# A decoder layer's middle stage: combination slots claimed early, three gate blocks kept on chip, the gating root by Newton steps, later key fetches and weights one step ahead

## The chip, the core and the metric

The kernel runs on one core of one Trainium2 chip. Its engines are TensorE (PE, with PEld for its weight loads), VectorE (DVE), ScalarE (ACT), GpSimd (POOL) and SyncE (SP), whose queue issues nearly all DMAs. The metric is the device time of one execution in microseconds (us), the median of several runs.

## What is computed

One layer of a decoder over 1024 prompt positions and 32 sample rows (8 sequences of 4), all in float32, width 1024. Shortened from the reference:

```python
h = layer_norm(ALPHA * x + 0.5 * swiglu(x, f1_w1, f1_w3, f1_w2), ln1_g, ln1_b)
z = h @ w_in + b_in                       # q, k, v, uv, ga, gb: 42 blocks of 128 columns
for g, (window, dil) in enumerate(ATT_GROUPS):      # (128,1), (512,4), (2048,16), 4 heads each
    o, lse = dilated_attn(q_g, k_g, v_g)
att = combine_groups(outs, lses)          # softmax over the three groups' lse, per head
u, vr = split(gelu(uv))                   # 512 columns each
vn = layer_norm(vr, sgu_ln_g, sgu_ln_b)   # these rows of the sample are an output too
yb = u * (tril(ws) @ vn + sgu_b)          # chunks of 128 positions, 4 channel groups
mix = (sigmoid(ga) * (att @ w_oa) + sigmoid(gb) * (yb @ w_ob)) @ w_out
h = layer_norm(ALPHA * h + mix, ln2_g, ln2_b)
h = layer_norm(ALPHA * h + 0.5 * swiglu(h, f2_w1, f2_w3, f2_w2), ln3_g, ln3_b)
```

Outputs are the two results, the key and value windows, and the normalised rows `vn` of the sample.

## The kernel before

Activations lie transposed, 128 channels on the partitions and 1056 positions along the row, cut into four chunks of 264 columns (`NC`, `C`). Every float32 matmul is made of three in a rounded format: high times high, high times low, low times high (`mm3`, L236; the matmul itself is L240). `split` makes the high half by a ScalarE copy (L251) and the low half by a VectorE subtraction (L252).

A tile framework orders the instructions of each engine. It traces the program in the order of the code, then schedules each engine with a machine model, by priorities that follow the code; `high_priority(offset=URGENT)` moves an instruction 300 places ahead, `issue_after` puts it behind another on its engine. Waits between engines are semaphores. Tiles come from pools with a fixed number of slots that are reused: `S` (37 slots of up to 1056 columns), `W` (8, weights), `M` (6, staging), `R` and `Q` (2 each, raw data), `X` (small ones), and in PSUM `mm` (3 banks) and `ax` (5). A tile holds a slot from its first use to its last. `held` (L105) takes an `S` tile and has GpSimd copy one element per partition into it at once (L108), so that it has its slot from then on.

Three work queues run beside the main loop: `bg` (attention), `slow` (the sample's attention, `sample`) and `mid` (gating and combination). They hold Python generators; `tick(n, m)` after each block of matmuls runs n steps of `bg`, m of `slow` and three (`MID`) of `mid`, always of the first generator in a queue, until it ends.

The stages are `ffn` (first SwiGLU), `widen` (the wide projection; spills its blocks to DRAM, `zD`), `mix`, and `ffn` again. The change is in `mix` and what it runs:

- The main loop computes the last ten of the gates' sixteen blocks, `n` = 6 to 15 (`gate8`, L984; 24 matmuls a chunk; ScalarE adds the bias into an `M` tile, L990; the tile is stored to `zD`, L991). For `n` = 6 to 12 each block's weights are fetched (`unit`, L214 to L223) and all four chunks done. The last three blocks are fetched together and only chunks 0 to 2 done; chunk 3 comes later in `beside` (L1588), to fill TensorE.
- `attend(i)` (`bg`) runs six steps, two head pairs by three groups. It fetches q, k, v (`fetch_qkv`, `fetch_z`, L1138), turns v (L1180), and over eight blocks does scores (PE L1200, DVE L1208, ACT L1212), turning (L1223, L1227) and values (L1239). It fetches the next step's q, k, v near its start. Its row minima and sums go to DRAM (`mlD`, L1265).
- `combine(hp)` (`mid`) after three steps reads these back (L1283 to L1289, `raw`), computes each group's factor (L1297 to L1310), writes it to DRAM (`cD`, L1312), reads it broadcast into three tiles `cbs` (L1319), and scales and adds the groups into `att` (L1324 to L1327).
- `sgu_norm` (`mid`) takes the statistics of the four `vr` blocks, the reciprocal root (`rsqrt`, L659 to L663), the scaling of nine tiles (L1483), and the sample's output rows (L1488 to L1490). `sgu_mix` makes the gated `yb` (L1507 to L1520).
- Then come `local(n)`, eight blocks of `yb @ w_ob` (`product`, multiplied on VectorE into the gate `mt[n]`, L1541), and the last loop, eight blocks of `att @ w_oa`, multiplied into the gate `ta[n]` that `fetch_gate` (L1580) reads back, added (L1633) and split. Weights are fetched by `narrow` (L225 to L234).

Of the kernel before, what the change touches and what calls it, by code (L numbers as in the profile page):

```python
# [21 lines left out]
P = 128  # L22
# [59 lines left out]
class Trunk:  # L82
# [1071 lines left out]
    def attend(self, i):  # L1154
# [19 lines left out]
        self.fetch_qkv(i + 1)  # L1174
# [97 lines left out]
    def combine(self, hp):  # L1272
        nc = self.nc
        t = []
        raw = self.S([16, 3, 2, P])
        for g in range(3):
            x = raw[:, g]
            for m in range(2):
                for h in range(2):
                    src = self.mlD[hp, g, m, h]  # L1280
                    o = x[8 * h : 8 * h + 8, m]
                    if g == 0:
                        nc.sync.dma_start(o, src.rearrange("(a x) -> a x", a=8))  # L1283
                    elif g == 1:
                        nc.sync.dma_start(
                            o.rearrange("p (r b) -> p r b", r=4), src.rearrange("(r a b) -> a r b", r=4, a=8)
                        )
                    else:
                        nc.sync.dma_start(  # L1289
                            o.rearrange("p (r b) -> p r b", r=16), src.rearrange("(r a b) -> a r b", r=16, a=8)  # L1290
                        )
# [22 lines left out]
        att = self.S([P, NT])  # L1314
        self.att[hp] = att
        cbs = [self.S([P, NP]) for _ in range(3)]
        for g, cb in enumerate(cbs):
            for h in range(2):
                nc.sync.dma_start(cb[64 * h : 64 * h + 64], self.cD[hp, g, h].partition_broadcast(64))  # L1319
        yield from self.pause(3)  # L1320
        for g, cb in enumerate(cbs):
            aT = self.attT.pop((hp, g))
# [113 lines left out]
    def sgu_norm(self):  # L1436
# [28 lines left out]
        for i in range(9):  # L1465
# [19 lines left out]
        v = self.M([NS, 512])  # L1485
        for op, k in ((ALU.mult, "sgu_ln_g"), (ALU.add, "sgu_ln_b")):
            t = self.M([NS, 512])
            nc.sync.dma_start(t, a[k].partition_broadcast(NS))  # L1488
            nc.vector.tensor_tensor(v, vn[4][:NS, 0] if op == ALU.mult else v, t, op=op)
        nc.sync.dma_start(a["svo"], v)  # L1490
        self.vn = vn
# [32 lines left out]
    def mix(self):  # L1524
# [18 lines left out]
        def local(n):  # L1543
            wb = self.narrow(a["wo"][n, :, 2 * P :], 4 * P)
# [12 lines left out]
        sgu = [self.sgu_norm()] + [self.sgu_mix(gg) for gg in range(4)]  # L1557
# [288 lines left out]
```

## Time and profile before

| what | us |
|---|---|
| median of 3 runs | 2202.6 |
| lowest and highest | 2198.51, 2202.74 |
| the profiled execution, its own time | 2202.1 |
| its span, first to last instruction | 2200.3 |

| engine | busy us | share of the span |
|---|---|---|
| PE | 2132.7 | 97% |
| PEld | 2093.7 | 95% |
| DVE | 1555.3 | 71% |
| ACT | 892.8 | 41% |
| POOL | 321.6 | 15% |

How to read the lines: in a timeline, a row has its start, its length, the engine, the line of the code, the operation, output and input tiles without their numbers and, in brackets, how long the engine was idle before it and what ended the wait. `x24` means that 24 alike in a row are merged. `SPq` is SP's own queue: such a row is the issue of a DMA, not its transfer. In a table of waits, the numbers are the total in us, how often, and the longest. A busy TensorE is not one at full speed: the granted clock stands beside it. A row of groups has the count, busy us and mean ns, then the idle time before them with its main causes.

### The profile page before, as it was taken

How to read it: one execution, taken by the hardware profiler on the slowest of the kernel's cores; microseconds unless marked ns; L12 is line 12 of the kernel's file. 1: busy time of each engine (PE TensorE's matmuls, PEld its weight loads, DVE VectorE, ACT ScalarE, POOL GpSimd, SP SyncE). 2: the span in 40 equal slices, each digit the busy share in tenths (PEclk: the TensorE clock that was granted, in tenths of full speed). 3: DMA queues.
4: the chain of work that ended last, by engine and by line, in shares of the span. 5: the costliest groups of instructions: out<-in, count | busy, mean ns of one | idle time of the engine just before them, and what ended most of it. 6: DMA issues, size and time to landing. Idle time of an engine off the chain costs nothing.

```text
span 2200.3 us, 43275 instructions
## 1 busy us (share of the span) xinstructions
PE 2132.7 (97%) x17305; PEld 2093.7 (95%) x17305; DVE 1555.3 (71%) x2724; ACT 892.8 (41%) x1681; POOL 321.6 (15%) x234
## 2 busy tenths in 40 slices
PE   9999999999998999999989988999999999999997
PEld 8999999999998999999879877999999999999997
DVE  8776776656788726787674647778576777656887
ACT  5444444421225634344465453245344444421224
POOL 0432332200010022232000000000332233100000
PEclk9999999999999999999999998999999999999998
DMA  4435545598973325666854637514354454597841
GB/s 157 146 134 178 176 161 175 194 372 319 329 279 134 136 101 193 205 219 222 312 166 151 186 119 244 195 41 143 129 185 156 166 185 159 181 393 290 303 183 79
DMA packets 170553, 429.01 MB, mean 195 GB/s; under 512 B 24864, under 2 KB 61584, under 8 KB 167664
## 3 DMA queue, kind: packets, MB, share of 16 engines
q1 hardware_dynamic: 169920, 425.71, 55.1%
q8 instruction: 135, 2.21, 0.4%
q14 instruction: 66, 0.54, 0.1%
q10 hardware_dynamic: 432, 0.54, 0.1%
HBM read 305.56 MB, written 166.81 MB: 215 GB/s over the span
## 4 chain that ended last, share of the span: by engine, by line
PE 83%; DMA 7%; DVE 6%; ACT 2%; issue 1%; SPq 1%; POOL 0%; ACTq 0%; DVEq 0%; POOLq 0%
PE ax L240 44%; PE mm L240 35%; DMA M<-kv 3%; DMA zD<-M 1%; DVE W L252 1%; PE ax L1200 1%; DMA S<-zD 1%; DVE X L1382 1%; PE ax L1223 1%; DVE S L252 1%; PE ax L1239 0%; DVE M L1392 0%; DVE S L627 0%; DVE M L1381 0%; DVE X L1397 0%
## 5 line engine op out<-in xcount | busy, mean ns | idle before, releaser
L240 PE MATMUL mm<-S,W 128*128 128x264 f32 x5208 | 694.8, 289 | 30.1 <-DVE S L1541 13.2
L240 PE MATMUL ax<-S,W 128*128 128x264 f32 x5400 | 706.9, 284 | 0.4 <-DVE W L252 0.2
L240 PEld LDWEIGHTS mm<-S,W 128*128 128x128 f32 x5208 | 659.2, 191 | 46.8 <-DVE S L1541 15.2
L240 PEld LDWEIGHTS ax<-S,W 128*128 128x128 f32 x5400 | 677.0, 188 | 2.7 <-ACT S L1030 0.8
L240 PE MATMUL ax<-S,S 128*128 128x264 f32 x3240 | 478.7, 285 | 4.0 <-DVE S L1039 3.9
L240 PEld LDWEIGHTS ax<-S,S 128*128 128x128 f32 x3240 | 429.6, 189 | 5.3 <-DVE S L1039 5.3
L240 PE MATMUL mm<-S,S 128*128 128x264 f32 x2472 | 383.8, 285 | 2.6 <-DVE S L252 2.0
L240 PEld LDWEIGHTS mm<-S,S 128*128 128x128 f32 x2472 | 333.7, 188 | 4.3 <-DVE S L252 2.2
L251 ACT CAST W<-R 128x1024 fp32r<-128x1024 f32 (+3 forms) x173 | 128.8, 761 | 319.7 <-PE mm L240 137.4
L382 POOL TENSOR_TENSOR Q<-R 128x512 f32<-128x512 f32 x49 | 70.3, 1434 | 798.2 <-DMA R<-w13a 202.8
L252 DVE TENSOR_TENSOR W<-R,W 128x1024 fp32r<-128x1024 f32 (+3 forms) x173 | 152.1, 883 | 26.7 <-ACT W L251 22.2
L251 ACT CAST W<-Q 128x1024 fp32r<-128x1024 f32 (+1 forms) x78 | 76.8, 984 | 224.2 <-POOL Q L383 89.4
L816 DVE SCALAR_TENSOR_TENSOR S<-ax,S 128x264 f32<-128x264 f32 x240 | 99.4, 427 | 66.8 <-PE ax L240 65.7
L457 DVE TENSOR_TENSOR S<-ax,M 128x264 f32<-128x264 f32 x82 | 32.8, 432 | 151.3 <-PE ax L240 151.3
L108 POOL CAST S<-ones 128x1 fp32r<-128x1 f32 x32 | 17.6, 571 | 751.4 <-DVE S L1633 363.5
L252 DVE TENSOR_TENSOR S<-Q,S 128x1024 fp32r<-128x1024 f32 (+1 forms) x78 | 112.6, 1444 | 3.8 <-ACT S L251 3.8
L252 DVE TENSOR_TENSOR W<-Q,W 128x1024 fp32r<-128x1024 f32 (+1 forms) x78 | 89.6, 1149 | 26.6 <-ACT W L251 26.6
L251 ACT CAST S<-Q 128x1024 fp32r<-128x1024 f32 (+1 forms) x78 | 76.8, 984 | 68.1 <-PE ax L240 49.7
L251 ACT CAST S<-R 128x512 fp32r<-128x512 f32 (+1 forms) x64 | 44.1, 689 | 105.9 <-DMA sumsA<-S 39.4
L252 DVE TENSOR_TENSOR S<-S,M 128x528 fp32r<-128x528 f32 x72 | 84.5, 1174 | 2.6 <-ACT M L251 0.8
L383 POOL TENSOR_TENSOR Q<-Q,R 128x512 f32<-128x512 f32 x49 | 81.0, 1653 | 2.7
L390 POOL TENSOR_TENSOR Q<-R,Q 128x512 f32<-128x512 f32 x49 | 80.5, 1644 | 1.1
(204 smaller groups left out, 2049.6 us busy)
## 6 DMA issues: line engine op xcount, KB each, us to landing
ws<-st SPq DMA_DIRECT2D x144, 256.0 KB
S<-sumsA SPq DMA_DIRECT2D x63, 528.0 KB
S<-sumsB SPq DMA_DIRECT2D x63, 528.0 KB
M<-kv SPq DMA_DIRECT2D x96, 256.0 KB
sumsA<-M SPq DMA_DIRECT2D x90, 264.0 KB
sumsB<-M SPq DMA_DIRECT2D x90, 264.0 KB
R<-w13b SPq DMA_DIRECT2D x44, 512.0 KB
R<-w13a SPq DMA_DIRECT2D x42, 512.0 KB
```

Source lines behind the costliest of these rows:

```text
L108: self.nc.gpsimd.tensor_copy(t[:, 0, :1] if len(shape) == 3 else t[:, :1], self.ones[:, :1])
L240: mm = lambda a, b, s, e: nc.tensor.matmul(o, a[:, cc], b, start=s, stop=e, skip_group_check=True)
L251: a = self.nc.scalar.copy(hi, src)
L252: b = self.nc.vector.tensor_tensor(lo, src, hi.bitcast(F32), op=ALU.subtract)
L382: tt(s12[:, lo], cd[:, lo], cd[:, hi], op=ALU.add)
L383: tt(s12[:, hi], s12[:, lo], ab[:, lo], op=ALU.subtract)
L390: tt(s34[:, hi], ab[:, hi], s12[:, hi], op=ALU.subtract)
L457: go(one, 5, False, lambda x: tt(h[:, x, 1], one[x], p7[:, x], op=ALU.add))
L816: nc.vector.scalar_tensor_tensor(y(x, r, e), bank[x], HALF, y(x, r, e), op0=ALU.mult, op1=ALU.add)
L1200: nc.tensor.matmul(pS[h][:, r, :nk], q[e, i * P : (i + 1) * P], k[e, k0 : k0 + nk], start=True, stop=True)
L1223: nc.tensor.transpose(pT[r][:, h, o], s[:, r, h, o], self.ident)
L1382: nc.vector.tensor_reduce(o, t, axis=AX.X, op=ALU.add)
```

## The change

- `attend`: the next step's q, k, v are fetched in the step of the fourth group of scores instead of near the start.
- `combine`: `raw`, `att` and the three `cbs` are taken with `held` at its start; the four loads of the first group become one.
- `sgu_norm`: two queue steps instead of one for each tile's statistics; the root by `rsqrt_dve` (L647 to L655: two VectorE operations, then three rounds of three) instead of ScalarE's square root, a reciprocal and one round. The sample's rows become a generator of their own, `sgu_rows`, at the end of the gating's queue, and use the free half of the last `vn` tile.
- `mix`, gates 6 to 12: weights are fetched one block ahead; two chunks share a staging tile and a store; the tile comes from `W` for blocks 6 to 11, from `M` for 12.
- `mix`, gates 13 to 15: `kept` tiles, taken with `held`, get the gates straight from PSUM and stay until the last loop uses them; nothing is stored or read back.
- Both product loops fetch their weights one step ahead (`wbs`, `was`).

```diff
 # attend
-        self.fetch_qkv(i + 1)
+        follower = i + 1
...
             if t < 4:
                 scores(t)
+            if t == 3:
+                self.fetch_qkv(follower)
 # combine
-        raw = self.S([16, 3, 2, P])
+        slot = self.held
+        raw = slot([P, 3 * 2 * P])[:16].rearrange("p (g m x) -> p g m x", g=3, m=2)
+        att, *cbs = [slot([P, NT]) for _ in range(4)]
...
+            src = self.mlD[hp, g]
+            if g == 0:
+                nc.sync.dma_start(x, src.rearrange("m h (a x) -> (h a) m x", a=8))
...
-        att = self.S([P, NT])
         self.att[hp] = att
-        cbs = [self.S([P, NP]) for _ in range(3)]
 # sgu_norm
-            yield
+            yield from self.pause(2)
...
-        self.rsqrt(rs[:, 0], rs[:, 1], mv[:, :, 1], EPS)
+        self.rsqrt_dve(rs[:, 0], rs[:, 1], mv[:, :, 1], mv[:, :, 1], EPS)
...
+    def sgu_rows(self):
+        nc, a = self.nc, self.a
+        v = self.vn[4][:NS]
         for op, k in ((ALU.mult, "sgu_ln_g"), (ALU.add, "sgu_ln_b")):
             t = self.M([NS, 512])
             nc.sync.dma_start(t, a[k].partition_broadcast(NS))
-            nc.vector.tensor_tensor(v, vn[4][:NS, 0] if op == ALU.mult else v, t, op=op)
-        nc.sync.dma_start(a["svo"], v)
+            yield from self.pause(2 * MID)
+            nc.vector.tensor_tensor(v[:, 1], v[:, 0 if op == ALU.mult else 1], t, op=op)
+        nc.sync.dma_start(a["svo"], v[:, 1])
 # mix
-            wb = self.narrow(a["wo"][n, :, 2 * P :], 4 * P)
+            wb = wbs.popleft()
+            if n + 1 < KB:
+                wbs.append(self.narrow(a["wo"][n + 1, :, 2 * P :], 4 * P))
...
-        for n in range(NLEAD, NLEAD + NTAIL - LAST):
-            w = self.unit(a["wzp"][n])
-            for c in (0, 2, 1, 3):
-                self.gate8(w, DENSE[n], c, AF.Identity, STEPS["tail"], 1)
-        units = {n: self.unit(a["wzp"][n]) for n in range(NLEAD + NTAIL - LAST, NLEAD + NTAIL)}
+        kept, end = {}, NLEAD + NTAIL - LAST
+        units = {NLEAD: self.unit(a["wzp"][NLEAD])}
+
+        def gate(n, c, *steps):
+            p = self.mm_tile()[:, :C]
+            self.dense8(p, units[n], c)
+            with self.urgent():
+                nc.scalar.activation(kept[n][:, c * C : c * C + C], p, AF.Identity, bias=self.bin(DENSE[n]))
+            self.tick(*steps)
+
+        for n in range(NLEAD, end):
+            w = units.pop(n)
+            for m in range(n + 1, n + 2 if n + 1 < end else NLEAD + NTAIL):
+                units[m] = self.unit(a["wzp"][m])
+                if m >= end:
+                    kept[m] = self.held([P, NT])
+            z = self.zD[DENSE[n]].rearrange("p (a b x) -> p b a x", a=2, b=2)
+            for b in range(2):
+                t = (self.W if n + 1 < end else self.M)([P, 2, C], F32)
+                for x in range(2):
+                    p = self.mm_tile()[:, :C]
+                    self.dense8(p, w, 2 * x + b)
+                    with self.urgent():
+                        nc.scalar.activation(t[:, x], p, AF.Identity, bias=self.bin(DENSE[n]))
+                    if x:
+                        nc.sync.dma_start(z[:, b], t)
+                    self.tick(STEPS["tail"], 1)
...
-                    self.gate8(units[n], DENSE[n], c, AF.Identity, STEPS["tail"], 1)
+                    gate(n, c, STEPS["tail"], 1)
...
+                m = NLEAD + NTAIL - KB + n + 3
+                ta.append(kept[m] if m in kept else self.fetch_z(29 + n))
...
             if n in BESIDE:
-                beside(BESIDE[n])
+                gate(BESIDE[n], NC - 1, 0, 0)
```

More of the change, by code (lines that the diff above doesn't have):

```diff
@@ L1484, in sgu_norm @@
             yield
-        v = self.M([NS, 512])
+        self.vn = vn
+    def sgu_rows(self):
+        nc, a = self.nc, self.a
+        v = self.vn[4][:NS]
         for op, k in ((ALU.mult, "sgu_ln_g"), (ALU.add, "sgu_ln_b")):
@@ L1614, in mix @@
         self.slow.append(sums)
+        wbs = deque([self.narrow(a["wo"][0, :, 2 * P :], 4 * P)])
         for n in range(KB):
             local(n)
+        was = deque([self.narrow(a["wo"][0, :, : 2 * P], 2 * P)])
         self.yb = None
-        ta = [fetch_gate(n) for n in range(3)]
+        ta = [self.fetch_z(26 + n) for n in range(3)]
         while self.bg or self.mid or self.slow[0] is not sums:
@@ L1637, in mix @@
             if n in BESIDE:
-                beside(BESIDE[n])
-        units = self.A = None
+                gate(BESIDE[n], NC - 1, 0, 0)
+        units = kept = self.A = None
         self.sqs, self.lns = {}, {}
```

43 lines of the change are left out of this document (13 added, 30 removed).

## The prediction

> **What bounds the kernel now.** I read the page first, then the busy time in three stretches, then what TensorE waited for in the middle one, then the timeline around each long wait.
>
> ```profile
> span 2200.3 us, 43275 instructions
> PE 2132.7 (97%) x17305; PEld 2093.7 (95%) x17305; DVE 1555.3 (71%) x2724; ACT 892.8 (41%) x1681; POOL 321.6 (15%) x234
> 0.00:1065.00 1065.00, 1050.05 (x8480) 1039.36 (x8481) 763.59 (x1218) 427.19 (x749) 199.69 (x146) 0.99 0.58 203
> 1065.00:1400.00 335.00, 297.64 (x2399) 270.98 (x2398) 209.04 (x549) 163.31 (x398) 1.38 (x3) 0.96 0.59 194
> 1400.00:2200.30 800.30, 785.05 (x6431) 783.34 (x6429) 582.65 (x959) 302.27 (x535) 120.49 (x85) 0.99 0.52 184
> ```
>
> The columns of the stretches are length, then busy time of PE, PEld, DVE, ACT, POOL, then granted clock, DMA share and GB/s. TensorE is the bound: it idles 67.6 us in all. The edits all lie in `mix`, which runs from 1065 to about 1400; there it idles 335.0 - 297.6 = 37.4 us, over half of all its idleness in 15% of the span, and at the lowest clock, 0.96. No edit takes a matmul away, so only these 37.4 us, and what a cold clock adds, can be won. Who held TensorE up in that stretch:
>
> ```profile
> PE mm L240 <- DVE S L1541: 13.2, 6, 10.7
> PE ax L1223 <- ACT S L1212: 11.2, 7, 5.9
> PE mm L240 <- ACT M L990: 4.9, 4, 3.0
> ```
>
> (total us, times, longest). Two single waits, 10.7 and 5.9, are nearly half.
>
> **The claimed slots and the longest wait.**
>
> ```profile
> 1315.13 1.26 SPq L1312 DMA_DIRECT2D cD<-S  x3
> 1316.82 3.04 SPq L1319 DMA_DIRECT2D S<-cD  x5
> 1319.91 2.00 SPq L1138 DMA_DIRECT2D S<-zD  x4
> 1321.96 0.45 SPq L1319 DMA_DIRECT2D S<-cD  x1
> 1321.90 1.23 DVE L1324 TENSOR_TENSOR S<-S,S 128x1024 f32<-128x1024 f32 x1 [6.17 <-DMA S<-cD]
> 1326.53 1.11 DVE L1541 TENSOR_TENSOR S<-S,mm 128x264 f32<-128x264 f32 x3 [0.68 <-DMA S<-zD]
> 1202.97 18.97 PE L240 MATMUL mm<-S,W 128*128 128x264 f32 x154
> 1327.01 27.65 PE L240 MATMUL mm<-S,W 128*128 128x264 f32 x204 [10.73 <-DVE S L1541]
> ```
>
> Three products of `local(4)` wait in PSUM for `mt[4]`. Its fetch (L1138) is marked urgent, yet it and three others stand in SP's queue right behind five of the six broadcast loads of `combine(1)` (L1319), which wait for that combination's own result (L1312). I read this as the slot pool giving out slots in the order of the code: `mt[4]` cannot be placed until the last factor tile `cbs[2]` is, and that tile is first touched by its load. A second place says the same: from 1202.97 TensorE runs 154 gate matmuls with no attention among them, while `combine(0)` waits for its factors. After the change all five tiles of a combination are claimed at its start by a GpSimd copy of one element per partition, so the fetches no longer stand behind the loads.
>
> The wait is worth 10.73 us plus a cold clock: 204 matmuls took 27.65, at the 18.97/154 = 0.123 us of the other row they take 25.1, so 2.5 more; 13.2 in all. Late next is VectorE, which sits 6.17 us before L1324 for the factor loads with the products queued behind it; three PSUM banks of 12 matmuls hold 3 x 12 x 0.123 = 4.4 us, leaving 1.8 exposed. **Gain 11** of bounds 0 (the order stays) to 13.2; I take the upper side, as nothing else delays these fetches.
>
> **The gating root.**
>
> ```profile
> 1120.07 1.28 ACT L659 ACT_TABLE_LOAD   x1
> 1124.47 6.46 ACT L1483 ACTIVATE S<-S,X 128x512 f32<-128x512 f32 x9 [0.27 <-DVE X L1479]
> 1130.95 1.28 ACT L1212 ACT_TABLE_LOAD   x1
> 1122.35 0.17 DVE L663 SCALAR_TENSOR_TENSOR X<-X 128x9 f32<-128x9 f32 x1
> 1127.24 0.08 DVE L1208 DVE_READ_ACCUMULATOR2_ANT X<- 128x1 f32 x1
> 1135.11 1.54 PE L1223 MATMUL ax<-ident,S 128*128 128x128 f32 x6 [5.88 <-ACT S L1212]
> 1143.14 0.82 PE L1223 MATMUL ax<-ident,S 128*128 128x128 f32 x6
> ```
>
> TensorE waits 5.88 us for exponentials whose scores VectorE had finished at 1127.3; ScalarE was in nine scalings back to back, then reloaded its exponential table, which the square root had thrown out. Out go the root, a reciprocal and two loads (2.56 us); in come eleven VectorE steps on 9 columns, 11 x 0.17 = 1.9 us instead of about 1.5 on the way to the scalings. Alone, that brings the exponentials 1.28 - 0.4 = 0.9 us forward. If the scalings are also dealt out between other ScalarE work (the statistics now take two steps each), the wait goes, and with it the cold clock behind it: the next four groups took 2.8 us more than their like (1.54 against 0.82 for the first). Bounds 0.9 to 8.7; **gain 5**, the middle, because the loop of the scalings itself keeps its step.
>
> The Trainium skill (ScalarE: Activation LUTs, What ACT_TABLE_LOAD costs) states 1283 ns for a load and about 1380 ns of drain beside it. The load agrees with 1.28, but the scalings end at 1130.93 and the load starts at 1130.95: no drain shows. By the page the two loads would be 5.3 us, and the gain some 2.8 larger.
>
> **The rows of the norm, and a blocked SP.**
>
> ```profile
> SPq L1488 <- DVE X L1208: 10.2, 1, 10.2
> 1143.89 0.93 PE L1200 MATMUL ax<-S,S 64*128 64x128 f32 x8
> 1150.07 0.88 PE L1223 MATMUL ax<-ident,S 128*128 128x128 f32 x6 [1.15 <-ACT S L1212]
> 1152.16 2.73 PE L1200 MATMUL ax<-S,S 64*128 64x128 f32 x8 [1.21 <-DVE M L1519]
> ```
>
> SP stood 10.2 us at the first factor load (L1488), waiting for an `M` tile, with the sample's key slabs queued behind it. Those slabs then came in a lump, and VectorE's work on them delays the scores: two waits of 1.2 us, and eight score matmuls at 2.73 instead of 0.93. The rows move behind the four mixings, into a half tile already there, with one `M` tile at a time. The moved step issues the same two loads, one store and two VectorE operations; SP and VectorE have room there, and POOL isn't passed. Bounds: 0 to 1.15 + 1.21 + 1.8 = 4.2. **Gain 2.5.**
>
> The Trainium skill (TensorE: Matmul & The Clock Gate, The HAM clock gate) has the clock halve only after an idle window of about 3.4 us. The slow rows behind gaps of 1.2 us speak against it, unless the window counts busy share rather than gaps; by the rule this term would lose its 1.8.
>
> **Staging outside `M`, three gates kept.**
>
> ```profile
> L990 ACT ACTIVATE M<-mm,cols 128x264 f32<-128x264 f32 x37 | 17.8, 480 | 31.7 <-DMA zD<-M 20.3 <-PE mm L240 4.8 <-issue 3.6
> L991 SPq DMA_DIRECT2D zD<-M x37: 319/325/688, 1076.0 to 1269.7; - x37
> SPq L991 <- ACT M L990: 57.1, 26, 8.3
> L1633 DVE TENSOR_TENSOR S<-S,S 128x1056 f32<-128x1056 f32 x8 | 10.0, 1251 | 0.0
> 1353.00:1391.00 38.00, 33.76 (x260) 31.86 (x259) 35.55 (x57) 18.31 (x24) 0.23 (x2) 1.00 0.63 208
> ```
>
> ScalarE waited 20.3 us for an `M` tile whose store had not landed, and TensorE 4.9 behind it; SP waited 57.1 at those stores. The 37 stores of 132 KB become 14 of 264 KB (12 from `W` tiles, two from `M`); nine vanish with the kept gates, and three fetches with them. ScalarE's 37 evictions stay. **Gain 5**: the 4.9 direct, and little more, bounds 0 to 4.9 + 4.2 (the waits for L1212 other than 5.88 and 1.15 come to 11.2 - 7.0; some of them follow from a ScalarE held up at a staging tile). In the last loop, VectorE is busy 35.6 of 38.0 us with the products, the adds (L1633) and their splits; saved fetches give at most its 2.4 us idle: **0.5**.
>
> **What it costs.**
>
> ```profile
> 1074.63 0.66 PE L1180 MATMUL ax<-ident,S 128*128 128x128 f32 x4 [1.66 <-DMA S<-zD]
> L108 POOL CAST S<-ones x32: 179/187/2625, 639.4 to 1488.5; 128x1 fp32r<-128x1 f32 x32
> ```
>
> The keys of the next attention step are fetched at the fourth group of scores instead of at the start: three slots come free for some 20 us, and the same three loads move behind other issues on SP. When such a fetch was last too late, TensorE waited 1.66 us; five moved fetches cost 0 to 8.3, and since at least nine steps of the background queue (three gates) still lie ahead of their use I take **0.5**. The thirteen claims take 0.19 us each on a GpSimd that does 1.4 us of work in the whole stretch; what hides them is that idleness, uncovered they would be 2.4. Their price is slots: five held from the start of a combination and three from unit 12 on. I take **1.5** for gates that wait for one, of 0 to the rival below. The weights of both product loops fetched one step ahead, the three merged loads of the first group's factors and the longer root chain lie beside TensorE's work: 0, covered for a weight by the four products of the step before it, 4 x 12 x 0.123 = 5.9 us; uncovered, each of the sixteen steps would wait for its load and split.
>
> **The sum.** 11 + 5 + 2.5 + 5 + 0.5 - 0.5 - 1.5 = 22.0. The profiled execution took 2202.1 us, 1.8 over its span and 0.5 under the shown median of 2202.6: 2202.1 - 22.0 = **2180**.
>
> **Rivals.**
>
> ```profile
> 1199.70 1.33 SPq L1283 DMA_DIRECT2D S<-mlD  x4
> 1215.83 0.28 DVE L1208 CUSTOM_DVE_ANT_0 S<-ax,M 128x128 f32<-128x128 f32 x1
> 1231.28 1.22 DVE L1327 TENSOR_TENSOR S<-S,S 128x1024 f32<-128x1024 f32 x1
> 1337.03 1.22 DVE L252 TENSOR_TENSOR S<-S,S 128x1024 fp32r<-128x1024 f32 x1
> 1348.82 0.43 DVE L1541 TENSOR_TENSOR S<-S,mm 128x264 f32<-128x264 f32 x1 [1.05 <-PE mm L240]
> ```
>
> *Slots run out, slower.* `combine(0)` takes from 1199.7 to 1232.5, 32.8 us. Counted in the code, 16 slots of normed halves, 8 of `yb`, 4 attention results, 3 keys and values and the 5 claimed are live then: 36 of 37, where one step of attention needs two, and the three kept gates queue behind. Before, attention paused from 1203.1, the end of its last scores, to 1215.8, 12.7 us. If it now pauses for all 32.8, the attention result, which was split at 1338.3, comes 20.1 later, at 1358.4, and the last local product, at 1348.8, no longer hides it: the last loop starts 9.6 us late, whatever was gained ahead of it, and the time is 2202.1 + 9.6 = 2212. It decides from a pause 10.5 us longer than before. For it speaks the count; against it that the later keys free three slots exactly there, and that gates fill TensorE meanwhile.
>
> *The longest wait only changes its name.* The fetches come early, but VectorE stands in front of L1324 as long, or the claims themselves are placed late: 11 of the 22 fall away, 2191. For it: 6.17 us of that wait are VectorE's own today.
>
> *It doesn't do what it says.* The claims queue on POOL behind those of the kept gates, so the fetches stay late, and the scalings stay in one lump: 5 + 0.5 + 0.9 - 2, about 4 us, 2198, which this kernel's measurement (0.2%, 4.4 us) cannot tell from no change.
>
> *More than forecast.* Of 37.4 us idle only the first fetch (1.66), the last loop and its end (5.4) stay, and 5.3 us of cold clock go: 2202.1 - 30.3 - 5.3 = 2166.
>
> **How the numbers follow.** Forecast (2170 to 2187) 0.45; half of it 0.20; more 0.10; no change 0.10; slower 0.15. So faster 0.75, same 0.10, slower 0.15. The range goes from 2163, a little under the best case, to 2204: it leaves out 0.03 below and most of the slow case above. The bounds of the single terms, 0 to 13.2, 0.9 to 8.7 and 0 to 9.1 above all, fill it.
>
> **What would show it.** Right: no wait of over 5 us for L1541 in the middle stretch, the urgent fetches ahead of the factor loads on SP, one table load fewer on each side of the scalings, no staging wait on ScalarE, TensorE idle there near 18 us. Wrong: attention away from TensorE for over 23 us around the first combination, waits for kept gates' evictions, VectorE idle before L1324 with TensorE idle beside it, or time lost outside `mix`, where nothing is changed and I expect the two runs alike.

## The result, and the profile after

Six runs of the changed kernel have a median of 2181.6 us (2173.3 to 2186.5), six of the kernel before 2201.4 us (2198.5 to 2204.1): ratio 0.9908, 95% interval 0.9887 to 0.9929. The profiled execution took 2182.69 us; the forecast was 2180. The total was right; the experiments show that three of its terms were not.

From the page of the changed kernel, the span and the engines' busy times:

```profile
span 2180.6 us, 43243 instructions
...
PE 2129.5 (98%) x17305; PEld 2090.8 (96%) x17305; DVE 1558.7 (71%) x2731; ACT 891.4 (41%) x1680; POOL 326.6 (15%) x247
```

and the same three stretches as before (length, busy time of PE, PEld, DVE, ACT, POOL, granted clock, DMA share, GB/s):

```profile
0.00:1065.00 1065.00, 1048.80 (x8481) 1037.41 (x8482) 764.84 (x1217) 425.78 (x747) 200.50 (x146) 1.00 0.58 203
1065.00:1400.00 335.00, 314.97 (x2563) 289.16 (x2562) 226.42 (x575) 166.12 (x400) 6.87 (x23) 0.97 0.60 198
1400.00:2180.60 780.60, 765.77 (x6265) 764.21 (x6264) 567.43 (x941) 299.51 (x533) 119.22 (x78) 0.99 0.51 184
```

TensorE is idle for 335.0 - 315.0 = 20.0 us of the middle stretch, 17.4 less than before; in the stretch ahead of it the idle time is nearly as it was (16.2 us, 15.0 before). What TensorE waits for there (total us, times, longest):

```profile
PE mm L240 <- DVE S L1544: 9.9, 9, 2.7
PE ax L1180 <- DMA S<-zD: 3.7, 1, 3.7
PE mm L240 <- ACT S L251: 2.7, 1, 2.7
PE ax L1223 <- ACT S L1212: 1.1, 1, 1.1
```

The waits of 10.7 and 5.9 us are gone, and so are those for the evictions of the gates. What is left stands at two places: one late fetch of keys (3.7), and the start of the last loop (most of the first row, and the third).

SP's order around the second combination, from the timeline:

```profile
1279.80 0.90 SPq L1138 DMA_DIRECT2D S<-zD  x2
...
1281.18 3.19 SPq L1138 DMA_DIRECT2D S<-zD  x4
1288.29 0.32 SPq L1267 DMA_DIRECT2D mlD<-X  x1
...
1294.61 0.36 SPq L1608 DMA_DIRECT2D Q<-wout  x1
1295.01 1.39 SPq L1138 DMA_DIRECT2D S<-zD  x3
1296.45 1.74 SPq L1289 DMA_DIRECT2D S<-mlD  x4
...
1311.52 1.26 SPq L1313 DMA_DIRECT2D cD<-S  x3
1314.62 3.68 SPq L1318 DMA_DIRECT2D S<-cD  x6
```

The urgent fetches of `mt` (L1138) now stand ahead of all six factor loads (L1318), as forecast. But the last four raw loads of the combination (L1289), which wait only for the store of the last attention step (L1267, 1288.29), go out at 1296.45, behind a load of `wout` and three fetches for the last loop.

Three moments describe the end of the stretch: the last transpose of attention (L1261, now L1263), the last add of the combination on VectorE (L1327, now L1326), and the first matmuls of the output projection (after L1650, now L1669). Before, from the timelines of TensorE and VectorE:

```profile
1302.83 0.27 PE L1261 MATMUL ax<-ident,X 128*32 128x128 f32 x1
1333.60 1.22 DVE L1327 TENSOR_TENSOR S<-S,S 128x1024 f32<-128x1024 f32 x1
1397.56 22.61 PE L240 MATMUL mm<-S,W 128*128 128x264 f32 x184 [1.23 <-DVE S L1650]
```

and after:

```profile
1284.29 0.27 PE L1263 MATMUL ax<-ident,X 128*32 128x128 f32 x1
1327.35 1.22 DVE L1326 TENSOR_TENSOR S<-S,S 128x1024 f32<-128x1024 f32 x1
1377.47 22.76 PE L240 MATMUL mm<-S,W 128*128 128x264 f32 x185 [0.89 <-DVE S L1669]
```

Attention ends 18.5 us earlier, the output projection begins 20.1 us earlier, and from there to the end both kernels need the same (2200.3 - 1397.6 = 802.7, 2180.6 - 1377.5 = 803.1). Between the two ends of the middle part something was gained and something given back: from attention to the combined result it is 32.0 us before and 44.3 after, and from there to the output projection 62.7 before and 48.9 after.

### The profile page after: what moved, and what is told of

The parts are those of the page before. It is cut to its first block, busy times and chain, and to the rows that moved or that the text cites. A ratio compares the mean times of both kernels' runs of the same rounds, so it can differ in the third digit from the quotient of the medians.

```text
span 2180.6 us, 43243 instructions
## 1 busy us (share of the span) xinstructions
PE 2129.5 (98%) x17305; PEld 2090.8 (96%) x17305; DVE 1558.7 (71%) x2731; ACT 891.4 (41%) x1680; POOL 326.6 (15%) x247
## 4 chain that ended last, share of the span: by engine, by line
PE 83%; DMA 7%; DVE 5%; ACT 2%; issue 1%; POOL 1%; SPq 0%; ACTq 0%; DVEq 0%; POOLq 0%
PE ax L240 45%; PE mm L240 35%; DMA S<-zD 2%; DMA M<-kv 1%; DMA R<-wz 1%; PE ax L1200 1%; PE ax L1239 1%; DVE W L252 1%; DVE S L252 1%; PE ax L1223 1%; DMA S<-hD 0%; DVE S L627 0%; DMA R<-wzp 0%; DVE S L1544 0%; ACT S L251 0%
## 5 line engine op out<-in xcount | busy, mean ns | idle before, releaser
L251 ACT CAST W<-R 128x1024 fp32r<-128x1024 f32 (+3 forms) x173 | 128.5, 761 | 301.8 <-PE mm L240 136.4
L252 DVE TENSOR_TENSOR W<-R,W 128x1024 fp32r<-128x1024 f32 (+3 forms) x173 | 155.5, 902 | 22.8 <-ACT W L251 22.2
L251 ACT CAST W<-Q 128x1024 fp32r<-128x1024 f32 (+1 forms) x78 | 76.7, 984 | 223.3 <-DVE Q L383 89.2
L252 DVE TENSOR_TENSOR S<-Q,S 128x1024 fp32r<-128x1024 f32 (+1 forms) x78 | 111.1, 1424 | 4.1 <-ACT S L251 3.8
L252 DVE TENSOR_TENSOR W<-Q,W 128x1024 fp32r<-128x1024 f32 (+1 forms) x78 | 90.5, 1160 | 24.4 <-ACT W L251 24.4
L251 ACT CAST S<-Q 128x1024 fp32r<-128x1024 f32 (+1 forms) x78 | 76.7, 984 | 68.5 <-PE ax L240 50.1
L251 ACT CAST S<-R 128x512 fp32r<-128x512 f32 (+1 forms) x64 | 44.0, 687 | 107.3 <-DMA sumsA<-S 40.4
L252 DVE TENSOR_TENSOR S<-S,M 128x528 fp32r<-128x528 f32 x72 | 84.5, 1173 | 3.0 <-ACT M L251 1.4
```

The lines of the kernel that those rows point to most:

```text
L251: a = self.nc.scalar.copy(hi, src)
L252: b = self.nc.vector.tensor_tensor(lo, src, hi.bitcast(F32), op=ALU.subtract)
```

## The experiments

The first four runs each put one part of the change back.

**The claims undone.**

```diff
-        slot = self.held
-        raw = slot([P, 3 * 2 * P])[:16].rearrange(...)
-        att, *cbs = [slot([P, NT]) for _ in range(4)]
+        raw = self.S([16, 3, 2, P])
...
+        att = self.S([P, NT])
         self.att[hp] = att
+        cbs = [self.S([P, NT]) for _ in range(3)]
```

> The changed kernel with one part put back: the tiles of a combination take their slots when their own loads first touch them, as before; the merged loads and all else stay. My theory (each wait has its own cause): the urgent fetches of mt stand behind the factor loads of the second combination again, TensorE waits once for over 5 us for a product of local (10.7 before), and the kernel takes 11 us more than the changed one, about 2193 us. Rival (the end of attention bounds the start of the last loop, so waits ahead of it only change places): the long wait comes back, but the waits at the start of the last loop, about 10.8 us in the changed kernel, shrink by as much; within 3 us of the changed kernel, 2182 to 2185.

2187.6 us, ratio 0.9939 (0.9916 to 0.9963): 6.0 us slower than the changed kernel by the medians, 6.8 by the ratios. SP's timeline shows the old picture again, five factor loads, four fetches, one factor load:

```profile
1301.19 3.05 SPq L1318 DMA_DIRECT2D S<-cD  x5
1304.28 2.02 SPq L1138 DMA_DIRECT2D S<-zD  x4
1306.51 0.45 SPq L1318 DMA_DIRECT2D S<-cD  x1
```

and TensorE's timeline the long wait, with another near the first combination:

```profile
1238.72 1.57 PE L1223 MATMUL ax<-ident,S 128*128 128x128 f32 x6 [6.55 <-ACT S L1212]
...
1311.69 27.20 PE L240 MATMUL mm<-S,W 128*128 128x264 f32 x204 [8.65 <-DVE S L1544]
```

With the claims undone the fetches stand behind the loads again, as slots handed out in the order of the code would have it. The price of 11 is not confirmed: these 8.65 us come back and the 6.55 us come on top, yet the kernel loses 6 to 7; the small waits at the start of the last loop go in return. The 6.55 us are a wait for scores: VectorE stands idle for 5.81 us before the first combination's first multiplication by its factors (L1323, 1236.15), and the scores (L1208) come behind it, at 1237.29. The truth lies between theory and rival.

**The root undone.**

```diff
-        self.rsqrt_dve(rs[:, 0], rs[:, 1], mv[:, :, 1], mv[:, :, 1], EPS)
+        self.rsqrt(rs[:, 0], rs[:, 1], mv[:, :, 1], EPS)
```

> The changed kernel with the square root of the gating norm put back on ScalarE (one root, one reciprocal), the statistics still two steps apart and the nine scalings dealt out as in the change. My theory of two halves: the root brings its table load and the reload of the exponential back, 2.56 us of ScalarE, but the wait of 5.88 us for L1212 came from the lump of scalings, so about 1 us comes back: 2182 to 2184, with one wait of 1 to 3 us for L1212. Rival (the table loads made the wait): 5 us or more slower, about 2187 to 2190, with the wait of near 5.9 us back and the clock at 0.93 from 1100 to 1200.

2185.1 us, ratio 0.9920 (0.9891 to 0.9948). 3.5 us slower by the medians, 2.6 by the ratios, which four runs cannot tell from the changed kernel. Behind the scalings the waits for L1212 are 0.8 and 2.2 us; a third, of 3.6 us, stands behind the last steps of the first combination (1255.44). The wait of 5.9 at the scalings does not come back with the square root. My expectation has the scalings dealt out in the change; they are not, as shown further down.

**The staging undone.**

```diff
-            for b in range(2):
-                t = (self.W if n + 1 < end else self.M)([P, 2, C], F32)
...
+            for c in (0, 2, 1, 3):
+                self.gate8(w, DENSE[n], c, AF.Identity, STEPS["tail"], 1)
```

> The changed kernel with the gates that are stored staged in M tiles of 264 columns again, 28 stores of 132 KB in the place of 14 of 264 KB; the three kept gates stay kept. My theory: ScalarE waits for M tiles again (20.3 us before, some 15 now with 28 of 37 stores) and TensorE 3 to 4 us behind it, 5 us slower: 2187. Rival (the waits of TensorE for staging only held up work that has slack before the end of attention): ScalarE's wait comes back, TensorE's time at the start of the last loop shrinks by as much, 2181 to 2183.

2196.7 us over ten runs, ratio 0.9975 (0.9961 to 0.9989): 15 us, three times the theory, the largest of the parts taken out. TensorE's waits in the stretch:

```profile
...
PE ax L1223 <- ACT S L1212: 7.6, 3, 4.9
PE mm L240 <- ACT M L990: 5.3, 3, 3.0
PE ax L1180 <- DMA S<-zD: 3.4, 3, 1.7
```

A wait of 4.9 us for exponentials stands here although root and spacing of the statistics are those of the change, but it is not the wait of before. It ends at 1150.01, and the scalings were done at 1138.7; the exponentials are late because their scores come from VectorE only at 1147.49, behind slabs of the sample (L1380, L1381) and a split of weights (L252). And the mechanism was not the one I had named: ScalarE itself waits only 2.4 us for an `M` tile here, not 15. What shows is the first attention step, on TensorE's timeline:

```profile
1075.43 0.66 PE L1180 MATMUL ax<-ident,S 128*128 128x128 f32 x4 [1.67 <-DMA S<-zD]
1075.84 3.16 PE L240 MATMUL mm<-S,W 128*128 128x264 f32 x24
1081.98 5.84 PE L240 MATMUL mm<-S,W 128*128 128x264 f32 x46 [2.97 <-ACT M L990]
...
1088.52 0.60 PE L1180 MATMUL ax<-ident,S 128*128 128x128 f32 x4
```

The second half of the step's transposes runs 13.1 us after the first, behind 70 gate matmuls and an eviction that is 3.0 us late. In the changed kernel it is 4.2 (1072.68 and 1076.89).

**The keys early again.**

```diff
+        self.fetch_qkv(i + 1)
-        follower = i + 1
...
-            if t == 3:
-                self.fetch_qkv(follower)
```

> The changed kernel with the keys, queries and values of the next attention step fetched at the start of a step again, in the place of the fourth group of scores. My theory: the wait of 3.74 us for the transposes of a step (L1180) and the cold clock behind it go, but three more slots are held during the first combination; the later fetch was costed at 0.5 us and the slots at 1.5, so the time is the same within 2 us: 2180 to 2184. Rival (the later fetch is what frees the slots for the claims and the kept gates): attention stops for more than 15 us around the first combination, 2190 or more.

2181.8 us, ratio 0.9909 (0.9883 to 0.9936): the same time, as the theory has it. The wait of 3.7 us is gone, and TensorE is idle for 14.5 us in the stretch instead of 20.0, without any gain in the runs. The profile shows where it goes: attention's first transposes start 6.7 us later than in the changed kernel (1079.38 against 1072.68), and from there to the output projection it takes 297.6 us instead of 304.8. So the stage is shorter, and what lies ahead of it is longer by as much. Whether the late start belongs to this kernel or to this one execution, one profile does not tell.

The next four runs separate staging from the pool it uses, and add one part to the kernel before.

**Pairs of columns, but in `M`.**

```diff
-                t = (self.W if n + 1 < end else self.M)([P, 2, C], F32)
+                t = self.M([P, 2, C], F32)
```

> The changed kernel with one letter changed: the pairs of gate columns are still stored together, 14 stores of 264 KB, but all of them are staged in M tiles, the pool that the attention's biases and the sample's slabs also use. Theory A (what counts is the pool: M is crowded, and a gate that waits there holds ScalarE, the exponentials and the scalings): the waits for L1572's kind of eviction and for L1212 come back, 2190 us or more, as with the staging undone (2196.7). Theory B (what counts is the number of stores, half as many): as the changed kernel, 2180 to 2185.

2188.8 us, ratio 0.9942 (0.9925 to 0.9958): 7 us slower than the changed kernel, 8 faster than with the single columns. Neither theory alone: by the times about half goes with the number of stores, half with the pool. The second half of the first transposes comes 11.1 us after the first (1073.69, 1084.74).

**Staging alone, on the kernel before.** The loop of the pairs as in the change; the last three gates are stored from `M` and read back as before.

```diff
-            for c in (0, 2, 1, 3):
-                self.gate8(w, DENSE[n], c, AF.Identity, STEPS["tail"], 1)
+            for b in range(2):
+                t = (self.W if n + 1 < end else self.M)([P, 2, C], F32)
...
```

> The kernel before with one part of the change: 28 gate columns staged as 14 pairs in weight tiles (the last two in M), units fetched one gate ahead; the last three gates are stored from M and read back as before, the square root, the claims and the keys as before. Theory after the first four runs (a ScalarE held up at a staging tile makes the waits for the exponentials too): the wait of 5.88 us for L1212 shrinks to under 3 though root and table loads stay, and 8 to 14 us are gained: 2188 to 2194. Rival, the term of the prediction: 5 us, 2196 to 2197, with the wait of 5.88 still there.

2199.6 us over ten runs, ratio 0.9991 (0.9981 to 1.0001): next to nothing, where taking the staging out of the changed kernel cost 15. The wait of 5.9 at the scalings is gone, as the theory says. Its place is taken later, on TensorE's timeline:

```profile
1242.11 1.12 PE L1223 MATMUL ax<-ident,S 128*128 128x128 f32 x4 [7.81 <-ACT S L1212]
...
1328.82 26.90 PE L240 MATMUL mm<-S,W 128*128 128x264 f32 x204 [10.88 <-DVE S L1541]
```

and the group of the last three gates' evictions on ScalarE (busy us, mean ns of one, idle us before them and what ended it):

```profile
L990 ACT ACTIVATE M<-mm,cols 128x264 f32<-128x264 f32 x9 | 4.3, 478 | 18.0 <-DMA zD<-M 17.0 <-PE ax L1223 1.0
```

Nine evictions of the three last gates wait 17.0 us for `M` tiles around the first combination, but TensorE waits for them for only 2.8 us (L990). The 7.8 us are another wait, as the timelines of ScalarE and VectorE show:

```profile
1240.96 0.51 ACT L1212 ACTIVATE S<-S,X 128x256 f32<-128x256 f32 x1 [7.37 <-DVE X L1208]
1233.85 1.23 DVE L1324 TENSOR_TENSOR S<-S,S 128x1024 f32<-128x1024 f32 x1 [4.66 <-DMA S<-cD]
```

ScalarE is idle for 7.37 us before these exponentials, waiting for scores; VectorE does those at 1240.50, behind the steps of the first combination, the first of which (L1324) waited 4.66 us for factors. It is the place of the 6.55 us of the run with the claims undone. That run has the kept gates, so these alone do not take such a wait away. Both lack the claims; with them VectorE stands there too (2.7 us in the changed kernel, 4.7 with the root undone), but TensorE's longest wait behind it is 3.6 us. No run has staging and claims alone. The long wait for `mt[4]` stands where it stood.

**Root and spacing alone; then the root alone.** Both on the kernel before; the first has also

```diff
-            yield
+            yield from self.pause(2)
```

behind each of the nine statistics.

> The kernel before with the gating root by Newton steps on VectorE and the statistics two steps apart, nothing else. Theory (staging makes that wait): ScalarE still stands at M tiles (20.3 us), a wait of 3 us or more for L1212 stays at the scalings, and the two table loads are all that is won: 1 to 3 us, 2198 to 2201. Rival, the term of the prediction: 5 us, 2196 to 2197, the wait gone.

> The kernel before with the gating root by Newton steps alone, the statistics one step apart as before. It tells the root from the spacing, which gained 8.4 us together by the times, while the profile shows the middle stretch only 1.7 us shorter and the stage ahead of it, where nothing differs, 5.8 us shorter. If the root is the cause: 8 us again, 2192 to 2195. If the table loads are all: 1 to 3 us, 2198 to 2200. If the gain came from the spacing: as before, 2200 to 2203.

With the spacing 2193.8 us, ratio 0.9962 (0.9949 to 0.9975), so 8.4 us; without it 2203.0 us over eleven runs, ratio 1.0009 (1.0000 to 1.0018). The Newton steps by themselves gain nothing, although they shorten the wait at the scalings from 5.9 to 5.1 us, near the 0.9 of the prediction; what the two gain comes with the spacing, which was not run by itself. With both, the wait at the scalings is down to 0.8 us, where the theory had 3 or more, and the gain is above what theory and rival had. The waits for staging tiles stay, as the theory says, and grow: TensorE waits 12.7 us for evictions into `M` (L990) instead of 4.9. What the spacing does to the scalings, from ScalarE's timeline of the changed kernel:

```profile
1120.59 0.86 ACT L1227 COPY S<-ax 128x512 f32<-128x512 f32 x2 [1.55 <-PE ax L1223]
1122.17 0.48 ACT L1588 ACTIVATE W<-mm,cols 128x264 f32<-128x264 f32 x1 [0.72 <-PE mm L240]
1122.55 5.75 ACT L1482 ACTIVATE S<-S,X 128x512 f32<-128x512 f32 x8
```

Eight of the nine scalings still run back to back, for 5.75 us. They are not dealt out at all: the lump stands at a place where the exponentials of a group are already done and turned (L1227 stands ahead of it, as it does with root and spacing alone, 1123.71 and 1125.76). Of the 8.4 us the one profile with root and spacing alone shows little inside the stretch: TensorE idles 36.6 us there, 37.4 before. Its first transposes start at 1068.78, 5.8 us earlier than before, and its output projection 7.6 us earlier (1390.01). I cannot attribute the 5.8, so the cause of most of this gain stays open.

**The claims alone.** The five tiles by `self.held` on the kernel before, nothing else.

```diff
-        raw = self.S([16, 3, 2, P])
+        slot = self.held
+        raw = slot([P, 3 * 2 * P])[:16].rearrange(...)
+        att, *cbs = [slot([P, NT]) for _ in range(4)]
```

> The kernel before with the five tiles of a combination claimed at its start, nothing else. Term of the prediction: 11 us, the wait of 10.73 us gone, 2190 to 2192. Rival, from the first claims run (undone they cost 6 us of time though a wait of 8.65 us came back): the waits at the start of the last loop take 4 to 8 us of it over, 2194 to 2198.

2196.2 us, ratio 0.9975 (0.9964 to 0.9986): 5.5 us, half of the term, as the rival says. The wait of 10.7 is gone; at the start of the last loop stand 2.1, 0.8, 0.9 and 3.1 us instead.

The three moments in all kernels, read from the same rows of each trace (us; "second half" is the distance between the two groups of transposes in the first attention step, and the column behind it the start of the first group):

| kernel | second half | first transposes | attention ends | combined after | output projection after |
|---|---|---|---|---|---|
| before | 13.1 | 1074.6 | 1302.8 | 32.0 | 62.7 |
| claims alone | 14.0 | 1072.5 | 1301.0 | 40.9 | 49.2 |
| staging alone | 4.2 | 1075.8 | 1303.1 | 34.3 | 60.2 |
| root and spacing alone | 13.1 | 1068.8 | 1295.3 | 33.5 | 61.2 |
| root alone | 13.1 | 1072.0 | 1300.7 | 33.5 | 60.1 |
| changed | 4.2 | 1072.7 | 1284.3 | 44.3 | 48.9 |
| claims undone | 4.2 | 1071.9 | 1288.2 | 31.4 | 60.5 |
| root undone | 4.2 | 1076.6 | 1290.2 | 43.9 | 48.6 |
| staging undone | 13.1 | 1075.4 | 1295.3 | 43.2 | 48.7 |
| pairs in `M` | 11.1 | 1073.7 | 1290.1 | 44.3 | 49.0 |
| keys early | 4.2 | 1079.4 | 1287.8 | 40.9 | 48.4 |

Two things stand out. The last column has two values: 60 to 63 without the claims, 48 to 49 with them. And the column ahead of it has two as well, 31 to 34 without and 41 to 44 with. The claims take 12 to 14 us out behind the combination and put 9 to 13 us into it. The rest lies in attention, but the moment at which it ends also holds what lies ahead of the stage, so it is counted from the first transposes. Attention then takes 228.2 us before, 226.6 to 228.7 in the four kernels with a part alone, and 211.6 with the whole change; with the claims undone 216.3, the root 213.6, the staging 219.9. No part that was run by itself shortens attention by even 2 us, and the whole change shortens it by 16.6. Some of that may be due to the parts that were never run by themselves; but taking one out costs 2 to 8 us of it, so the parts work together.

From that came a version that puts the second combination first, and two more.

**The combination first.**

```diff
-        mn = self.X([16, P], "cmin", 1)
+        with self.tc.high_priority(offset=2 * URGENT):
+            mn = self.X([16, P], "cmin", 1)
...
-        ta = [self.fetch_z(26 + n) for n in range(3)]
+        with self.tc.issue_after(self.raw):
+            ta = [self.fetch_z(26 + n) for n in range(3)]
...
-        split_att()
+        with self.tc.high_priority(offset=URGENT):
+            split_att()
```

`self.raw` is the last raw load of the combination.

> The changed kernel with the second combination put ahead of what now stands before it: the fetches of the first three gates of the last loop are issued behind its raw loads, its small VectorE steps and the split of the attention results have priority over the products of local. Theory (attention's end and the combination behind it set the start of the last loop: in ten kernels the output run began 89 to 94 us after the last step of attention): the combination takes 5 to 8 us less from the end of attention (27.2 us to its factor stores in the changed kernel, 12.3 in the one before), the waits of 2.7, 1.6, 1.2 and 2.7 us at the start of the last loop shrink, 2175 to 2178 us. Rival (the local products set that start): they wait for VectorE instead, 2180 to 2184.

2176.8 us (2175.7 to 2177.7), ratio 0.9892 (0.9879 to 0.9906): 4.8 us faster than the changed kernel by the medians, 3.5 by the ratios, whose intervals overlap, and 24.7 faster than the kernel before. Its slowest run lies below five of the six of the change. Its combination takes 40.4 us (1282.95 to 1323.38), 3.9 less than in the changed kernel and not the 5 to 8 of the theory, and the output projection follows 49.3 us later; the two halves of the start of the last loop, changed kernel first:

```profile
1300.00:1325.00 25.00, 20.32 (x159) 19.41 (x157) 15.82 (x33) 6.91 (x9) 0.00 (x0) 0.97 0.69 197
1325.00:1350.00 25.00, 18.80 (x125) 17.45 (x126) 22.51 (x37) 11.03 (x15) 0.00 (x0) 0.82 0.47 147
```

and with the combination first:

```profile
1300.00:1325.00 25.00, 19.77 (x152) 18.63 (x150) 18.73 (x36) 8.44 (x12) 0.00 (x0) 1.00 0.70 201
1325.00:1350.00 25.00, 20.57 (x157) 19.12 (x156) 22.99 (x41) 10.89 (x15) 0.00 (x0) 1.00 0.63 205
```

TensorE's idle time is nearly the same, 10.9 against 9.7 us, in eleven gaps of at most 1.5 us instead of nine of up to 2.7. What differs is the clock, 1.00 instead of 0.82, and with it 157 matmuls instead of 125 in the second half.

**The combination first, and keys at the second group.** The `t == 3` of the key fetch becomes `t == 1`.

> As v1, and the keys of the next attention step are fetched at the second group of scores instead of the fourth. Theory: the wait of 3.74 us for the transposes of a step (L1180) goes, attention ends some 3 us earlier, and since attention's end bounds, so does the kernel: 2172 to 2175. Rival, as fetched at the start of a step (2181.8 against 2181.6): no gain over v1, whatever TensorE's waits say.

2178.7 us, ratio 0.9902 (0.9887 to 0.9917): no gain, as the rival says. Attention ends at 1280.9 instead of 1283.0, but it also began earlier: from its first transposes it takes 209.0 us (from 1071.85), against 206.3 without this edit (from 1076.62).

**Attention started earlier.**

```diff
-        yield from self.pause(2 if i else 8)
+        yield from self.pause(2)
```

> The changed kernel with the first attention step started six background steps (two gate products, about 3 us) earlier; the same work, the same waits allowed. Theory (attention's end bounds the middle stretch): all six steps and the end of attention move 3 us forward and the kernel gains 2 to 3 us, 2178 to 2180, though no wait of TensorE is taken away. Rival (TensorE's idle time bounds): the same time, 2181 to 2183.

2181.4 us, ratio 0.9916 (0.9902 to 0.9929): the same time. Attention does end 5.2 us earlier, at 1279.1, but the combination now takes 48.2 us, so its result is there at 1327.3 instead of 1328.6. SP's timeline shows what holds it:

```profile
1282.41 0.73 SPq L1267 DMA_DIRECT2D mlD<-X  x1
1296.39 2.38 SPq L1289 DMA_DIRECT2D S<-mlD  x4
```

The store of the last attention step goes out 5.9 us earlier than in the changed kernel, and the last four raw loads go out when they did there (1296.45), again behind loads of `wout` and fetches for the last loop. My theory, that attention's end bounds, falls in this form: here the combination waits for its turn in SP's queue, its result comes hardly earlier, and the last loop starts no earlier either. This version has the time of the changed kernel and was run beside the version with the combination first: each of its four runs (2180.5 to 2184.5) is slower than each of that version's (2175.7 to 2177.7).

## Why the prediction was right, and where it was not

**The total** of 22.0 against 19.8 by the medians is right because errors of its terms cancel, as far as the terms were run: the claims gave 4 to 6 us less than forecast, the staging 10 more in the changed kernel. That is luck. The first error is one of kind: the terms were added as if each wait were paid for by itself. The runs point to a chain, attention, second combination, last loop, and a part is worth what it moves that chain. Of the 20.1 us by which the output projection begins earlier, attention's length gives 16.6, and no part that was run alone gave even 2 of them. Three parts added alone to the kernel before gave 5.5, 8.4 and 2.0 us; taken out of the changed kernel, two of them cost 6.8 and 15.

**The claimed slots, 11.** The mechanism was right in each step (slots in the order of the code, the fetches stuck behind the factor loads, the claim moves them). The step that failed is "leaving 1.8 exposed", with "nothing else delays these fetches" behind it. I asked what is late next for the product that waits, and found VectorE before L1324. I did not ask what the four fetches and the running products now stand in front of: the combination's own raw loads and small VectorE steps, which took 32.0 us when the products of `local` stood still, and take 44.3 now. In the place of 1.8 us TensorE has waits of 2.7, 1.6, 1.2 and 2.7 us between 1318.9 and 1329.8, 8.2 in all. The part measured 5.5 to 6.8.

**The gating root, 5.** The prediction gave 0.9 of it to the root alone and the rest to scalings dealt out among other work. The first half holds (nothing measurable). The second named the wrong mechanism: the lump of scalings stays, its place moves. The term was too small by up to 3 us on the kernel before, if the 8.4 are all its own, which the profile does not show, and the root's own share in the changed kernel is too small to be told. Of the table loads, the two at the scalings go, but L1554, L1304 and L1648 load at 1292.31, 1304.45 and 1329.72, where there was one: the exponentials of the second combination now fall among the sigmoids of the gates. ScalarE's timeline:

```profile
1304.45 1.28 ACT L1304 ACT_TABLE_LOAD   x1 [0.60 <-DVE S L1303]
...
1328.66 1.04 ACT L251 CAST S<-S 128x1024 fp32r<-128x1024 f32 x1 [9.34 <-DVE S L1326]
1329.72 1.28 ACT L1648 ACT_TABLE_LOAD   x1
```

There are four loads in the stretch as before, and the one at 1304.45 lies on the combination. The prediction did not look there. By the Trainium skill's drain beside a load (ScalarE: Activation LUTs, What ACT_TABLE_LOAD costs) each would cost about 1.38 us more; as before, none shows: L251 ends at 1329.70, the load starts at 1329.72.

**Staging outside `M`, 5.** Mis-sized by three: 15 us when it is taken out. "The 4.9 direct, and little more" was read off who released TensorE. But with single columns in `M` the first attention step is late as well (second half after 13.1 us instead of 4.2), attention takes 219.9 us instead of 211.6, and scores that come late from VectorE cost TensorE 4.9 us for exponentials. The bound of 9.1 was too low as well. On the kernel before, without the claims and the kept gates, the staging is worth 2. There it takes away the wait at the scalings, which I had booked under the root and which root and spacing alone take away too, so it can be earned only once; and TensorE waits 7.8 us for scores at the first combination instead. The kept gates, which the prediction counted with half a microsecond, no run has alone.

**Keys later, 0.5, and slots, 1.5.** For the keys right: 0.2 us. The one late fetch costs TensorE 3.7 us, more than the 1.66 that the prediction had as the price of one, and the runs do not show it in the time. Attention did not pause longer at the first combination: its third and fourth step end 39.1 us apart (1180.9 and 1220.0), 54.5 before (1198.2 and 1252.7). The rival of the slots did not happen; their 1.5 has no run of its own.

**The rivals.** "The longest wait only changes its name" was half true: the claims gave half of their 11. The staging gave more than its term and made up for it. "More than forecast" counted all of TensorE's idle time as to be won; the run with early keys has 5.5 us less of it and the same time.

**The signs.** Right: no wait of over 5 us for the products (2.7 the longest), the fetches ahead of the factor loads, one table load fewer on each side of the scalings, staging waits of ScalarE down from 20.3 to 0.2 us, 20.0 us idle against "near 18", and the rest of the kernel alike. One of the wrong signs came too: VectorE idle before L1324 (now L1323) with TensorE idle beside it (timelines of VectorE and TensorE):

```profile
1319.86 1.23 DVE L1323 TENSOR_TENSOR S<-S,S 128x1024 f32<-128x1024 f32 x1 [3.73 <-DMA S<-cD]
1321.57 0.61 PE L240 MATMUL mm<-S,W 128*128 128x264 f32 x3 [2.69 <-DVE S L1544]
```

VectorE stands from 1316.1 to 1319.9 and TensorE from 1318.9 to 1321.6, until the product behind L1323 is done. It belongs to the rival by which the longest wait only changes its name, and half of the term went that way.

**Not tried:** the rows of the norm, the kept gates, and the weights one step ahead by themselves. The 2.5 us of the rows is unconfirmed; of the wait of 10.2 us that SP had at their loads, waits of 3.3 and 1.5 are left (L1491).

## What to carry to other kernels

Where background work feeds the next stage, mark its milestones in the trace (first step, last step, result ready, next stage begins), count them from the first, and compare them over variants; they show what the list of TensorE's waits does not, that one part takes out what another has put in. When a fetch is moved ahead of a blocked queue, ask what the fetch, and the work that it sets free, now stands in front of. Test a part both ways, added to the kernel before and taken out of the kernel after: where the two differ, the parts depend on each other, and a sum of terms is not a forecast.

## What the runs showed of the hardware

In this trace the clock halved without one long gap. Changed kernel, slices of 2 us at the start of the last loop:

```profile
1320.00:1322.00 2.00, 0.43 (x3) 0.42 (x3) 1.42 (x2) 0.00 (x0) 0.00 (x0) 1.00 1.03 227
1322.00:1324.00 2.00, 0.40 (x3) 0.22 (x2) 1.56 (x2) 0.00 (x0) 0.00 (x0) 0.89 1.03 242
1324.00:1326.00 2.00, 0.81 (x3) 0.49 (x3) 1.60 (x3) 0.00 (x0) 0.00 (x0) 0.50 0.73 297
...
1332.00:1334.00 2.00, 2.00 (x12) 2.00 (x11) 1.98 (x4) 1.08 (x1) 0.00 (x0) 0.55 0.00 0
1334.00:1336.00 2.00, 2.00 (x18) 1.99 (x17) 2.00 (x4) 0.41 (x1) 0.00 (x0) 1.00 0.32 61
```

By the share of each slice the clock fell to a half at about 1323.6. Until then TensorE had had a gap of 2.7 us, three matmuls of 0.6 us in all, and most of a gap of 1.6: idle for 4.1 of the 4.7 us from 1318.9. Neither gap is as long as the idle window of about 3.4 us of the Trainium skill (TensorE: Matmul & The Clock Gate, The HAM clock gate). The clock stayed at a half until about 1333.8, some 3 us after TensorE was busy again at 1331.0. This fits the prediction's reading, that such a window counts busy share; it is one place, and no run was made to test it. Eleven gaps of at most 1.5 us at a busy share of 0.8 (the version with the combination first) left the clock at 1.00.

Profiles of the variants differ ahead of the edited stage too: over thirteen of them (the version with attention started earlier left out) the first transposes of attention begin between 1068.8 and 1079.4 us. With one profile for each kernel it stays open how much of that belongs to the kernel and how much to the execution. A difference of a few microseconds between two profiles is to be read from moments inside the stage, and the time of the kernel from medians.
